# Hybrid decoder block on one core: paired latent tiles, projection norms' roots on GpSimd, and a new load order before the MLP

## The chip, the cores and the metric

One Trainium2 chip, one core of it. The metric is device time in microseconds of one execution; 2975.97 us is the median of 3 runs of the kernel before (2975.77 to 2978.42). Below, TensorE is the matmul engine (PE in the rows, PEld its weight loads), DVE is VectorE, ACT is ScalarE, POOL is GpSimd, and SP issues most loads. DVE and ACT read PSUM, where TensorE writes; GpSimd reads and writes SBUF alone.

## The reference

A transformer block on x of 2048 tokens by 1024, float32, in this order:

- `h = rmsnorm(x, attn_norm_g)`; `proj = h @ w_in`, 2216 columns: the queries, keys and values of 8 Fox heads (3 x 512), 8 forget gates, the query latent c_q (384), the key/value latent c_kv (256), and a rotary key (32).
- Fox: causal attention with a decay bias made from the cumulative sum of `log_sigmoid` of the gates.
- MLA: `c_q` and `c_kv` are normalised (`rmsnorm` over 384 and 256), then multiplied by `w_uq` and `w_ukv`, giving queries, keys and values of 8 heads of 64, and rotary parts of 32; causal attention.
- Both results are normalised and joined; `x = x + mixed @ w_o`.
- `x = x + square(relu(rmsnorm(x) @ w_up)) @ w_down`, 4096 wide, then a final `rmsnorm`.

An rmsnorm needs `1/sqrt(mean(x*x) + eps)` for each token: here "the root".

## The kernel before

**Precision.** Every float32 operand of a matmul is split in a high part and a rest (`split_ps`, `split_w`, `split_to`), and a product is three matmuls (`mm3`, lines 126 to 128): high x high, high x rest, rest x high. Large products are done by seven half-size products of sums instead of eight (names S1 to S4 and T1 to T4 are such sums).

**Slots.** SBUF holds 16 tiles of 8 KB a partition ("big", `s8`) and 21 of 4 KB ("mid", `s4`). Taking a slot takes the one that has been free longest; what writes it first waits for its last reader. PSUM holds four tiles of two banks each (`bank2`).

**Stages.** The projection runs in two rounds of 1024 tokens (p = 0, 1). In each: `prep` normalises an x tile of 128 tokens (squares on ACT, root, scaling on DVE at line 334) and its `turn` transposes it on TensorE (line 339) and splits it. Eight query latents (`latent` with w_cq) and, after the MLA queries, eight key/value latents (with w_ck, 296 columns that include the rotary key and the gates, copied to `krf` at line 389). A latent is 24 matmuls; squares on ACT (385), the root, scaling on DVE out of PSUM (387), and, three `mm3` later, a transpose (394) and a split. Then MLA keys and values (`mla_rows`, `mla_v`), the rotary keys and, in round 1, the gates. Between the latents, `step()` puts halves of the T sums on GpSimd (532, 543). Then `fox`: 21 products, whose last seven (c = 2) in round 0 bring along the eight `prep` of round 1.

After the attention, `fetch` reads a tile of the joined result, and 16 tiles are multiplied by w_o (lines 1087 to 1117; `seq` takes them in pairs from two halves). Each tile ends in a norm, and two of them are turned (`turn`, 1007) and made into the operands of the up products, some kept, some stored in DRAM (`xd`) and loaded again (`x_load`). `x_split` splits such an operand, `up_load` and `up_prep` load and split w_up.

**The root** (`rstd`, 77 to 88): DVE scales and adds eps (79), GpSimd takes the power -1/2 (81), and four DVE instructions (83 to 87) do one Newton step.

**Order.** Each engine runs its own list in order. The lists are made by a planner from a simulated timeline: among instructions that are ready it takes the earliest written. `pin` keeps an instruction behind the one written before it on its engine; the T sums on GpSimd and some splits are pinned. `later(n, f)` runs f after n more `mm3`, and `flush` runs what is due.

Of the kernel before, what the change touches and what calls it, by code (L numbers as in the profile page):

```python
# [18 lines left out]
P = 128  # L19
# [26 lines left out]
def block_kernel(ctx, tc, x, positions, attn_norm_g, w_in, b_forget, q_norm_g, w_uq, kv_norm_g, w_ukv,  # L46
# [30 lines left out]
    def rstd(ssq, n, w=1, tag=""):  # L77
# [9 lines left out]
        nc.vector.tensor_tensor(r, y, t, ALU.mult)  # L87
        return r
# [164 lines left out]
    with ExitStack() as es:  # L253
# [17 lines left out]

        def load_g_att():
            g = s4.get([P, D], F32)
            nc.sync.dma_start(g, attn_norm_g.broadcast_to([P, D]))
            return g
# [52 lines left out]
        def prep(X, t):  # L328
# [5 lines left out]
            nc.vector.scalar_tensor_tensor(xt, xt, rstd(ssq, D, tag="x"), g_att, ALU.mult, ALU.mult)  # L334
# [15 lines left out]
        def load_latent(*cols, early=False):  # L350
# [3 lines left out]
            for half in range(2):  # L354
                hi, lo = s8.get([P, 4, n]), s8.get([P, 4, n])
                parts.append((hi, lo))
                for k in (0, 2):
# [4 lines left out]
                    if early:  # L362
                        nc.scalar.activation(hi[:, k:k + 2], raw, AF.Copy)
                        nc.gpsimd.tensor_tensor(lo[:, k:k + 2], raw, f32v(hi[:, k:k + 2]), ALU.subtract)
                    else:
                        split_w(hi[:, k:k + 2], lo[:, k:k + 2], raw)
# [12 lines left out]
        def latent(X, t, w, n, nn, gain, dst):  # L379
            j, i = t // 4 % 2, t % 4  # L380
            ps = bank2()[:, 0]
            mm3(ps[:, 0:nn], lambda k: [a[:, k % 4, tk(i)] for a in X[f"B{k // 4 + 1}{j + 1}"]],
                lambda k: [a[:, k % 4] for a in w[k // 4]], KD)
            ssq = sml.tile([P, 1], F32, name="ssq")
            nc.scalar.activation(junk_c[:, 0:n], ps[:, 0:n], AF.Square, accum_out=ssq)
            cn = s4.get([P, n], F32)
            nc.vector.scalar_tensor_tensor(cn, ps[:, 0:n], rstd(ssq, n), gain, ALU.mult, ALU.mult)
            if nn > n:
                nc.vector.tensor_copy(krf[:, t], ps[:, n:nn])  # L389

            def turn():
                tp = bank2()[:, 0]
                for k in range(n // P):
                    nc.tensor.transpose(tp[:, tk(k)], cn[:, tk(k)], ident)
                split_ps(dst[0][:, :, tk(i)], dst[1][:, :, tk(i)], tp[:, 0:n].rearrange("p (k s) -> p k s", s=P))
                s4.put(cn)
            later(DEFER_C, turn)
            flush(False)
# [255 lines left out]
        wcq = load_latent((OFF_CQ, RQ), early=True)  # L654
# [3 lines left out]
        def ahead(p, c, i):  # L658

            nonlocal wcq, g_att, first  # L660
            if c < 2:
                return
            if p == 0:
                if i == 0:
                    g_att = load_g_att()
                elif i in (1, 3):
                    prep_operands(Xn, i // 2)
                while turns and i < 6:
                    turns.pop(0)()
                if 1 <= i < 1 + 4:  # L670
                    turns.extend(prep(Xn, 8 + 2 * (i - 1) + n) for n in range(2))
                if i == 5:
# [7 lines left out]
        for p in range(2):  # L680
# [5 lines left out]
            for i in range(8):  # L686
                if p == 0:
# [5 lines left out]
                    if i == 0:  # L693
                        load_constants()
# [3 lines left out]
                latent(X, 8 * p + i, wcq, RQ, RQ, g_q, cq[i // 4])  # L698
# [19 lines left out]
            for i in range(8):  # L718
                latent(X, 8 * p + i, wck, RKV, 296, g_kv, ck[i // 4])
# [14 lines left out]
            mla_rows(g0, ck[0], 2, wk, mk, None)  # L734
            flush()
            for n in range(2):
# [3 lines left out]
            split_operand(X, raws, "T1")  # L740
            mla_rows(g0 + 1, ck[1], 2, wk, mk, None)
            s4.put(*wuk)
            fox_prep(0)
            mla_v(g0, ck[0], wuv)
            s4.put(*ck[0])
# [234 lines left out]
    def fetch(t, first):  # L980
        mt = s4.get([P, KD, P], F32)
        nc.sync.dma_start(mt, mixT.rearrange("(k p) s -> p k s", p=P)[:, :, tk(t)])
        sq = s4.get([P, KD, P], F32)
# [7 lines left out]
        st = [mh, ml]  # L991
# [95 lines left out]
    for n, t in enumerate(seq):  # L1087
        st = cur.pop()
        mh, ml, r2 = st
# [510 lines left out]
```

## Time and profile before

| | |
|---|---|
| median of 3 runs | 2975.97 us |
| the profiled execution | 2976.84 us, its span 2975.0 us |
| TensorE busy | 2825.9 us, 95% of the span |
| DVE, ACT, GpSimd busy | 2276.2, 1399.4, 1350.0 us |
| bytes moved by DMA | 442.96 MB, 149 GB/s |
| granted TensorE clock, mean | 0.979 |

A share of the span is a mean over stages with different limits: in attention and in the MLP TensorE is hardly ever idle, and the idle time lies in the projection, at the start, and around the MLP's first products. The granted clock is given as a share of full speed (2.4 GHz); the lower level is half of it.

### The profile page before, as it was taken

Reading aid. Unit: us, or ns where it says so; the run is one execution under the profiler, and the core shown is the slowest. Engines: PE = TensorE matmul, PEld = TensorE weight load, DVE = VectorE, ACT = ScalarE, POOL = GpSimd, SP = SyncE. Lnnn points to the kernel's source line nnn. Section 1 sums busy time; section 2 is a strip of 40 time slices with the busy share of each in tenths; the row PEclk is TensorE's granted clock in tenths of the full one; section 3 lists DMA queues with packets and bytes.
Section 4 is the critical chain, followed back from the end, with each engine's and each line's share of the span. In section 5 each row is a group of like instructions: output and inputs, shape, how many; then the busy total and the mean of one; then the engine's idle time right before and its main releaser. Section 6 shows DMA issues by size and latency. Waiting matters only on the chain. (4 is left out here: it accounts for less than half of the span.)

```text
span 2975.0 us, 40707 instructions
## 1 busy us (share of the span) xinstructions
PE 2825.9 (95%) x14634; PEld 2375.9 (80%) x14634; DVE 2276.2 (77%) x3317; ACT 1399.4 (47%) x2485; POOL 1350.0 (45%) x896
## 2 busy tenths in 40 slices
PE   7799979999999999999899889999999999999998
PEld 7778968878888888887778778888888788878886
DVE  7867686588888888888757666658666678897998
ACT  4144223477877777787533323223222433344432
POOL 3624252355445545547623235556555433453321
PEclk9999989999999999999999999999999999999999
DMA  5364535834434335331245654455444844465551
GB/s 140 127 217 161 162 108 174 254 90 105 94 89 112 85 91 118 79 90 59 62 146 184 209 197 156 156 211 220 158 152 150 292 153 153 139 219 190 205 191 57
DMA packets 262521, 442.96 MB, mean 149 GB/s; under 512 B 41712, under 2 KB 150384, under 8 KB 255600
## 3 DMA queue, kind: packets, MB, share of 16 engines
q1 hardware_dynamic: 206848, 300.75, 34.3%
q10 hardware_dynamic: 55472, 139.61, 12.4%
q8 instruction: 116, 1.90, 0.3%
q14 instruction: 85, 0.70, 0.1%
HBM read 275.54 MB, written 156.37 MB: 145 GB/s over the span
## 5 line engine op out<-in xcount | busy, mean ns | idle before, releaser
L1257 PE MATMUL mm<-big,mid 128*128 128x512 f32 x2688 | 619.7, 392 | 17.9 <-DVE mid L1038 7.2
L1257 PEld LDWEIGHTS mm<-big,mid 128*128 128x128 f32 x2688 | 505.9, 189 | 130.6 <-ACT big L1332 10.3
L128 PE MATMUL mm<-big,mid 128*128 128x512 f32 x1312 | 513.9, 393 | 7.9 <-DVE mid L237 6.2
L821 PE MATMUL ps_s<-big,big 96*128 96x384 f32 (+11 forms) x1720 | 447.8, 381 | 3.4 <-ACT mid L827 3.4
L127 PE MATMUL mm<-big,big 128*128 128x512 f32 (+2 forms) x1160 | 436.4, 376 | 0.6 <-DVE big L237 0.6
L126 PE MATMUL mm<-big,big 128*128 128x512 f32 (+2 forms) x1072 | 404.4, 377 | 12.3 <-DVE krf L389 9.8
L847 POOL TENSOR_SCALAR mid<-mid,rl,fac 128x768 f32<-128x768 f32 (+4 forms) x256 | 257.8, 1017 | 288.1 <-DVE rl L844 149.5
L826 DVE TENSOR_REDUCE negm<-ps_s 128x1 f32<-128x896 f32 (+7 forms) x384 | 348.3, 908 | 47.7 <-PE ps_s L821 42.9
L243 POOL TENSOR_TENSOR mid<-mid,mid 128x1024 f32<-128x1024 f32 x88 | 237.8, 2702 | 294.6 <-DVE mid L577 94.9
L236 ACT ACTIVATE big<-mid 128x1024 fp32r<-128x1024 f32 x218 | 214.9, 1049 | 319.9 <-PE mm L127 200.5
L827 ACT ACTIVATE mid<-ps_s,negm 128x896 f32<-128x896 f32 (+7 forms) x384 | 332.3, 866 | 50.4 <-DVE negm L826 42.2
L867 PE MATMUL ps_t<-ident,mid 128*128 128x128 f32 x2176 | 341.5, 275 | 4.0 <-POOL mid L847 2.9
L867 PEld LDWEIGHTS ps_t<-ident,mid 128*128 128x128 f32 x2176 | 276.0, 142 | 58.5 <-POOL mid L847 3.1
L821 PEld LDWEIGHTS ps_s<-big,big 96*128 96x128 f32 (+2 forms) x1720 | 291.2, 194 | 20.8 <-ACT mid L827 7.8
L1168 POOL TENSOR_TENSOR mid<-mid,mid 128x1024 f32<-128x1024 f32 x60 | 197.6, 3320 | 230.6 <-DVE big L237 217.2
L128 PEld LDWEIGHTS mm<-big,mid 128*128 128x128 f32 x1312 | 248.1, 189 | 61.2 <-DVE mid L237 7.1
L237 DVE TENSOR_TENSOR mid<-mid,mid 128x1024 fp32r<-128x1024 f32 x112 | 206.1, 1865 | 116.0 <-ACT mid L236 79.7
L94 DVE TENSOR_TENSOR big<-ps_t,big 128x512 fp32r<-128x512 f32 (+3 forms) x427 | 254.4, 602 | 36.6 <-ACT big L93 33.3
L93 ACT ACTIVATE big<-ps_t 128x512 fp32r<-128x512 f32 (+3 forms) x427 | 224.7, 534 | 108.5 <-PE ps_t L867 105.0
L127 PEld LDWEIGHTS mm<-big,big 128*128 128x128 f32 x1160 | 220.9, 190 | 36.5 <-DVE big L237 1.0
L126 PEld LDWEIGHTS mm<-big,big 128*128 128x128 f32 x1072 | 204.1, 190 | 47.0 <-DVE krf L389 10.8
L126 PE MATMUL mm<-big,mid 128*128 128x512 f32 x528 | 210.6, 399 | 7.1 <-ACT mid L988 3.2
(213 smaller groups left out, 5188.3 us busy)
## 6 DMA issues: line engine op xcount, KB each, us to landing
gd<-mid ACTq DMA_DIRECT2D x109, 512.0 KB, 3.0
mid<-gd SPq DMA_DIRECT2D x109, 512.0 KB, 3.6
mid<-in_w_up SPq DMA_DIRECT2D x64, 512.0 KB, 5.3
mid<-in_w_down SPq DMA_DIRECT2D x64, 512.0 KB, 5.1
mid<-in_x SPq DMA_DIRECT2D x32, 512.0 KB, 3.6
xd<-mid ACTq DMA_DIRECT2D x28, 512.0 KB, 3.4
big<-xd SPq DMA_DIRECT2D x14, 1024.0 KB, 8.4
mid<-in_w_in SPq DMA_DIRECT2D x24, 512.0 KB, 4.6
```

The source lines that it names most:

```text
L93: nc.scalar.activation(hi, ps, AF.Copy)
L94: nc.vector.tensor_tensor(lo, ps, f32v(hi), ALU.subtract)
L126: nc.tensor.matmul(ps, lh, rh, start=(k == 0), stop=False)
L127: nc.tensor.matmul(ps, lh, rl, start=False, stop=False)
L128: nc.tensor.matmul(ps, ll, rh, start=False, stop=(k == nk - 1))
L243: (eng or nc.gpsimd).tensor_tensor(t, raws[a], raws[b], op)
L821: nc.tensor.matmul(ps[:, i, 0:wm], l[0:rows, qs], r[0:rows, kb:kb + wm], start=(n == 0), stop=(n == len(ops) - 1))
L826: nc.vector.tensor_reduce(negm[:, j, c:c + 1], src, AX.XY, ALU.max, negate=True)
L827: nc.scalar.activation(prob[:, 0:w].rearrange("p (b w) -> p b w", b=nb), src, AF.Exp, bias=negm[:, j, c:c + 1], accum_out=lsum[:, j, c:c + 1])
L847: nc.gpsimd.tensor_scalar(pr, pr, rl, 1.0 if nch == 1 else fac[:, j, c:c + 1], ALU.mult, ALU.mult)
L867: nc.tensor.transpose(ps[:, j * P:(j + 1) * P], prob[:, kt * P - k0:(kt + 1) * P - k0], ident)
L1257: nc.tensor.matmul(ps[:, m], l[:, k, tk(m)], r[:, :, tk(k)], start=(first and k == n == 0), stop=(k == 3 and n == 2), skip_group_check=True)
```

## The change

- `rstd_pool` does all six instructions of a root on GpSimd. It is used for the x tiles of round 1 (t > 7) and for the latents. The tiles of round 0 and all later norms keep `rstd`.
- `latent` works on pairs: two tiles fill the two halves of one PSUM tile. After the second, ACT copies both halves to an SBUF slot, squares them from there and copies the rotary part to `krf`; one `rstd_pool` of two columns; two scalings on DVE in SBUF; and one `turn` for both, three `mm3` later (eight for the last pair of the key/value latents).
- The first weights are split by ACT and DVE, and after the first two x tiles; before, by ACT and GpSimd, at once.
- The gain and the x tiles of round 1 are loaded in the Fox products c = 1, i = 5 and 6 and then a step ahead of their `prep`.
- `mla_v` of the first half goes ahead of the rotary keys, the gates and `mla_rows` of the second half; the split of T1 and `fox_prep(0)` move with it.
- At w_o, the x tile is loaded in `fetch`, one tile earlier. `up_load(0)` goes from tile 13 to 14; B21's load from tile 11 to the middle of tile 15, when two of the four weight pairs have been given back; the split of T2 from behind the loop to tile 10.

```
+    def rstd_pool(ssq, n, w=1, tag=""):
+        op = nc.gpsimd
+        v, y, t, r = (sml.tile([P, 4], F32, name=f"rp_{c}{tag}")[:, 0:w] for c in "vytr")
+        op.tensor_scalar(v, ssq, 1.0 / n, EPS, ALU.mult, ALU.add)
+        op.tensor_tensor(y, v, mhalf[:, 0:w], ALU.pow)
+        op.tensor_tensor(t, y, y, ALU.mult)
+        op.tensor_tensor(t, t, v, ALU.mult)
+        op.tensor_scalar(t, t, -0.5, 1.5, ALU.mult, ALU.add)
+        op.tensor_tensor(r, y, t, ALU.mult)
+        return r
...
+        def fetch_x(*ts):
+            for t in ts:
+                xts[t] = load_x(t)
...
-            nc.vector.scalar_tensor_tensor(xt, xt, rstd(ssq, D, tag="x"), g_att, ALU.mult, ALU.mult)
+            nc.vector.scalar_tensor_tensor(xt, xt, (rstd_pool if t > 7 else rstd)(ssq, D, tag="x"), g_att, ALU.mult, ALU.mult)
...
-                    if early:
-                        nc.scalar.activation(hi[:, k:k + 2], raw, AF.Copy)
-                        nc.gpsimd.tensor_tensor(lo[:, k:k + 2], raw, f32v(hi[:, k:k + 2]), ALU.subtract)
+                    if splits is None:
+                        split_w(hi[:, k:k + 2], lo[:, k:k + 2], raw)
                     else:
-                        split_w(hi[:, k:k + 2], lo[:, k:k + 2], raw)
+                        splits.append(lambda hi=hi[:, k:k + 2], lo=lo[:, k:k + 2], raw=raw: split_to(hi, lo, raw))
...
+        pair = []
+
+        def latent(X, t, w, n, nn, gain, dst, defer):
             j, i = t // 4 % 2, t % 4
-            ps = bank2()[:, 0]
...
+            a = t % 2
+            if a == 0:
+                pair[:] = [bank2()]
+            ps, = pair
+            mm3(ps[:, a, 0:nn], lambda k: [b[:, k % 4, tk(i)] for b in X[f"B{k // 4 + 1}{j + 1}"]],
+                lambda k: [b[:, k % 4] for b in w[k // 4]], KD)
+            if a == 0:
+                flush(False)
+                return
+            raw = s4.get([P, 2, 512], F32)
+            cn = raw[:, :, 0:n]
+            nc.scalar.activation(raw[:, :, 0:nn], ps[:, :, 0:nn], AF.Copy)
+            ssq = sml.tile([P, 2], F32, name="ssq")
+            for b in range(2):
+                nc.scalar.activation(junk_c[:, 0:n], cn[:, b], AF.Square, accum_out=ssq[:, b:b + 1])
             if nn > n:
-                nc.vector.tensor_copy(krf[:, t], ps[:, n:nn])
+                nc.scalar.activation(krf[:, t - 1:t + 1], raw[:, :, n:nn], AF.Copy)
+            r = rstd_pool(ssq, n, 2)
+            for b in range(2):
+                nc.vector.scalar_tensor_tensor(cn[:, b], cn[:, b], r[:, b:b + 1], gain, ALU.mult, ALU.mult)
...
-            later(DEFER_C, turn)
+            later(defer, turn)
...
+            if p == 0 and c == 1 and i > 4:
+                if i == 5:
+                    g_att = load_g_att()
+                else:
+                    fetch_x(8, 9)
...
+                    if i < 4:
+                        fetch_x(8 + 2 * i, 9 + 2 * i)
...
                     if i == 0:
+                        for f in splits:
+                            f()
                         load_constants()
...
-                latent(X, 8 * p + i, wck, RKV, 296, g_kv, ck[i // 4])
+                latent(X, 8 * p + i, wck, RKV, 296, g_kv, ck[i // 4], DEFER_C if i < 7 else 8)
...
             mla_rows(g0, ck[0], 2, wk, mk, None)
+            split_operand(X, raws, "T1")
+            mla_v(g0, ck[0], wuv)
             flush()
+            s4.put(*ck[0])
             for n in range(2):
                 rotary_keys(g0 + n)
             if p:
                 forget_gates()
-            split_operand(X, raws, "T1")
+            fox_prep(0)
             mla_rows(g0 + 1, ck[1], 2, wk, mk, None)
             s4.put(*wuk)
-            fox_prep(0)
-            mla_v(g0, ck[0], wuv)
-            s4.put(*ck[0])
...
     def fetch(t, first):
+        xt = s4.get([P, D], F32)
+        nc.sync.dma_start(xt, x[tk(t), :])
...
-        xt = s4.get([P, D], F32)
-        nc.sync.dma_start(xt, x[tk(t), :])
+        if n == 14:
+            up_load(0)
...
+            if n == 15:
+                for w in wo[2 * g:2 * g + 2]:
+                    s8.put(*w)
+                if g == 0:
+                    x_load(0, "B21")
...
-        if n == 11:
-            x_load(0, "B21")
-        if n == 13:
-            up_load(0)
+        if n == 10:
+            x_split(0, "T2")
...
-    for w in wo:
-        s8.put(*w)
     up_prep(0, 2)
-    x_split(0, "T2")
```

## Rows read from the trace of the kernel before

**Rows 1.** The page: busy time by engine, one group, one DMA issue (KB, us to landing).
```profile
PE 2825.9 (95%) x14634; PEld 2375.9 (80%) x14634; DVE 2276.2 (77%) x3317; ACT 1399.4 (47%) x2485; POOL 1350.0 (45%) x896
...
L93 ACT ACTIVATE big<-ps_t 128x512 fp32r<-128x512 f32 (+3 forms) x427 | 224.7, 534 | 108.5 <-PE ps_t L867 105.0
...
big<-xd SPq DMA_DIRECT2D x14, 1024.0 KB, 8.4
```

**Rows 2.** Waits of TensorE, whole span: us in total, times, longest.
```profile
PE mm L126 <- DVE krf L389: 24.6, 6, 7.4
PE mm L339 <- DVE mid L334: 17.3, 3, 8.9
...
PE mm L1257 <- DVE mid L1038: 7.2, 1, 7.2
...
PE mm L126 <- ACT mid L93: 6.0, 2, 4.7
...
PE mm L394 <- DVE mid L94: 4.9, 4, 1.5
PE mm L339 <- DVE rs_vx L79: 4.0, 1, 4.0
```

**Rows 3.** Table of stretches: length, busy us by engine, granted clock, DMA share, GB/s.
```profile
85.00:152.00 67.00, 50.88 (x299) 45.29 (x298) 54.66 (x97) 13.29 (x32) 39.34 (x24) 0.87 0.43 141
365.00:446.00 81.00, 59.34 (x320) 51.24 (x320) 67.05 (x129) 20.03 (x43) 42.07 (x25) 0.85 0.38 128
255.00:300.00 45.00, 39.00 (x309) 38.38 (x308) 37.63 (x72) 22.38 (x39) 20.53 (x18) 0.92 0.54 171
```

**Rows 4.** Groups on DVE, 92 to 146 us: busy us, mean ns, idle before.
```profile
L83 DVE TENSOR_TENSOR rs_t<-rs_y 128x1 f32<-128x1 f32 x8 | 15.9, 1982 | 2.8 <-POOL rs_y L81 2.7
...
L387 DVE SCALAR_TENSOR_TENSOR mid<-mm,rs_r,mid 128x256 f32<-128x256 f32 x8 | 3.9, 482 | 0.3
```

**Rows 5.** Groups on GpSimd, whole span.
```profile
L532 POOL TENSOR_TENSOR big<-big,big 128x1024 f32<-128x1024 f32 x16 | 38.1, 2385 | 0.0
...
L81 POOL TENSOR_TENSOR rs_y<-rs_v,mhalf 128x2 f32<-128x2 f32 x16 | 14.3, 891 | 60.8 <-DVE rs_v L79 60.8
...
L847 POOL TENSOR_SCALAR mid<-mid,rl 128x128 f32<-128x128 f32 x16 | 5.9, 370 | 12.9 <-DVE rl L835 12.9
```

**Rows 6.** Timeline of DVE at the start: start us, us, idle before in brackets.
```profile
6.76 0.16 DVE L83 TENSOR_TENSOR rs_tx<-rs_yx 128x1 f32<-128x1 f32 x1 [0.68 <-POOL rs_yx L81]
...
7.54 1.28 DVE L334 SCALAR_TENSOR_TENSOR mid<-mid,rs_rx,mid 128x1024 f32<-128x1024 f32 x1
...
10.25 1.78 DVE L83 TENSOR_TENSOR rs_tx<-rs_yx 128x1 f32<-128x1 f32 x1 [0.67 <-POOL rs_yx L81]
...
15.60 2.79 DVE L334 SCALAR_TENSOR_TENSOR mid<-mid,rs_rx,mid 128x1024 f32<-128x1024 f32 x1
...
29.42 1.02 DVE L104 TENSOR_TENSOR mid<-mid,mid 128x768 fp32r<-128x768 f32 x1
```

**Rows 7.** Timeline of GpSimd at the start.
```profile
10.21 7.10 POOL L364 TENSOR_TENSOR big<-mid,big 128x768 fp32r<-128x768 f32 x4
```

**Rows 8.** Timeline of TensorE: at the start, and after the latents of round 0.
```profile
18.44 1.97 PE L339 MATMUL mm<-ident,mid 128*128 128x128 f32 x8 [7.60 <-DVE mid L334]
...
127.72 0.30 PE L126 MATMUL mm<-big,big 128*128 128x296 f32 x1
...
129.64 0.30 PE L128 MATMUL mm<-big,big 128*128 128x296 f32 x1
...
140.94 0.80 PE L126 MATMUL mm<-mid,mid 128*128 128x512 f32 x1 [7.40 <-DVE krf L389]
...
144.94 0.55 PE L126 MATMUL mm<-mid,mid 128*128 128x512 f32 x1
```

**Rows 9.** Timeline of ACT in the last Fox products of round 0.
```profile
258.21 1.06 ACT L333 ACTIVATE junk<-mid 128x1024 bf16<-128x1024 f32 x1 [2.94 <-DMA mid<-in_x]
```

**Rows 10.** Timeline of DVE on the way into the MLP.
```profile
1688.66 4.48 DVE L237 TENSOR_TENSOR big<-big,big 128x2048 fp32r<-128x2048 f32 x2
```

More of the change, by code (lines that the diff above doesn't have):

```diff
@@ L348, in block_kernel, with load_latent @@
         ukv = w_ukv.rearrange("(k p) (h d) -> p k h d", p=P, d=2 * HD)
-        def load_latent(*cols, early=False):
+        def load_latent(*cols, splits=None):
             n = sum(c[1] for c in cols)
@@ L377, in load_heads @@
             return hi, lo
-        def latent(X, t, w, n, nn, gain, dst):
+        pair = []
+        def latent(X, t, w, n, nn, gain, dst, defer):
             j, i = t // 4 % 2, t % 4
-            ps = bank2()[:, 0]
[L382 to L387, printed above, removed]
+            a = t % 2
[13 more added lines that the diff above has]
+                nc.scalar.activation(junk_c[:, 0:n], cn[:, b], AF.Square, accum_out=ssq[:, b:b + 1])
@@ L388, in latent @@
             if nn > n:
-                nc.vector.tensor_copy(krf[:, t], ps[:, n:nn])
+                nc.scalar.activation(krf[:, t - 1:t + 1], raw[:, :, n:nn], AF.Copy)
+            r = rstd_pool(ssq, n, 2)
+            for b in range(2):
+                nc.vector.scalar_tensor_tensor(cn[:, b], cn[:, b], r[:, b:b + 1], gain, ALU.mult, ALU.mult)
             def turn():
-                tp = bank2()[:, 0]
-                for k in range(n // P):
-                    nc.tensor.transpose(tp[:, tk(k)], cn[:, tk(k)], ident)
@@ L395, in turn @@
-                split_ps(dst[0][:, :, tk(i)], dst[1][:, :, tk(i)], tp[:, 0:n].rearrange("p (k s) -> p k s", s=P))
-                s4.put(cn)
-            later(DEFER_C, turn)
+                tp = bank2()
+                for b in range(2):
+                    for k in range(n // P):
+                        nc.tensor.transpose(tp[:, b, tk(k)], cn[:, b, tk(k)], ident)
+                s2 = slice((i - 1) * P, (i + 1) * P)
+                split_ps(*[d[:, :, s2].rearrange("p k (b s) -> p b k s", b=2) for d in dst],
+                         tp[:, :, 0:n].rearrange("p b (k s) -> p b k s", s=P))
@@ L398, in latent @@
+                s4.put(raw)
+            later(defer, turn)
             flush(False)
@@ L652, in fox @@
             s8.put(uv, gs)
-        wcq = load_latent((OFF_CQ, RQ), early=True)
+        splits = []
+        wcq = load_latent((OFF_CQ, RQ), splits=splits)
         Xn, turns = {}, []
@@ L663, in ahead @@
             if p == 0:
-                if i == 0:
-                    g_att = load_g_att()
-                elif i in (1, 3):
+                if i in (1, 3):
                     prep_operands(Xn, i // 2)
@@ L697, in block_kernel @@
                         turns.pop(0)()
-                latent(X, 8 * p + i, wcq, RQ, RQ, g_q, cq[i // 4])
+                latent(X, 8 * p + i, wcq, RQ, RQ, g_q, cq[i // 4], DEFER_C)
                 if i == 3:
@@ L990, in fetch @@
         s4.put(mt)
-        st = [mh, ml]
+        st = [mh, ml, xt]
         def stats():
@@ L1088, in block_kernel @@
         st = cur.pop()
-        mh, ml, r2 = st
+        mh, ml, xt, r2 = st
         if n + 1 < NT:
             cur.append(fetch(seq[n + 1], False))
-        xt = s4.get([P, D], F32)
-        nc.sync.dma_start(xt, x[tk(t), :])
+        if n == 14:
+            up_load(0)
         for g in range(2):
```

## The prediction, made before the changed kernel was run

> **What bounds the kernel now.** I read the page first, then the waits of TensorE, then a table by stage, then the engines' timelines around the longest waits. On the page TensorE is busy for 2825.9 us of 2975.0, DVE for 77% [rows 1]; the reader is to see that at most 149 us of idle TensorE can be won, and that no matmul is taken out here. The view of waits says where the idle time lies [rows 2]. Its first line, 24.6 us in six waits, is a projection matmul that waits for the DVE copy into krf: the last reader of the PSUM tile that the matmul is to write. The next, 17.3 us in three, is the transpose of a normalised x tile that waits for DVE, nearly all of it at the start of the kernel. Both stand in stretches that the change rewrites. The table by stage [rows 3] shows it from the other side: in the two stretches around the key/value latents (85 to 152 us and 365 to 446 us) TensorE is busy for 50.88 of 67 and 59.34 of 81 us, at granted clocks of 0.87 and 0.85, while DVE is busy for 54.66 and 67.05. DVE is late there, though not with its own work: in the first round, the first product of the reciprocal root (128x1) takes 1982 ns on average [rows 4], nearly as long as the GpSimd add of 2385 ns [rows 5] that runs beside it, where the same form takes 0.16 us at 6.76 us, with GpSimd idle [rows 6].
>
> The profiled execution took 2976.84 us, 1.84 us around its span; the median of the runs shown is 0.87 us lower. The sum is made against the execution and moved by 0.87 at the end.
>
> **Part 1, the start.** Before, GpSimd subtracts the four low parts of the first weights in one block of 7.10 us [rows 7]. The second x tile goes from L83 to the end of L334 from 10.25 to 18.39, 8.14 us; the first, beside an idle GpSimd, from 6.76 to 8.82, 2.06 us [rows 6]. The change puts the four subtractions on DVE, behind the two tiles. The block goes and with it 6.1 us of delay. In its place DVE has four subtractions at 1.02 us (the 128x768 form at 29.42 [rows 6]), 4.1 us, half of which I let TensorE's first tile hide, since it takes the weights part by part. Late next is DVE with these low parts. Between 0 (all on the path, and the splits of x behind them) and 7.6 (the wait itself [rows 8]) I take 4.5.
>
> **Part 2, the query latents.** Per tile DVE loses five small instructions, and TensorE hardly waits there. Between -2 and +2: 1.
>
> **Part 3, the key/value latents, two rounds.** Removed: the waits 24.6 (krf), 4.9 (transposes for DVE) and 6.0 (rows for ACT), 35.5 us in all [rows 2]. ACT now copies both halves of a paired PSUM tile at once, and a 512-wide read of PSUM takes it 534 ns [rows 1]; so the tile no longer waits for the norm. With the waits goes slow clock: after the wait that ends at 140.94, nine matmuls take 4.00 us [rows 8] where the later spacing of 0.24 us would take 2.1 (512 columns, from the 296-column spacing below); 1.9 us each for some three such waits in the two rounds, 6 us (bounds 3.8 and 9.5, two and five waits).
>
> Added: a chain that is longer for a pair. ACT copies and squares, three instructions at up to 0.53, about 1.7 us. GpSimd then does six small instructions: the power at 891 ns [rows 5], and five for which the nearest row is the 128x128 scaling, 370 ns, so 2.7 us (at 0.1 us each it would be 1.4). GpSimd also has two pinned adds per pair, 4.8 us, each placed behind the roots in front of it. A pair costs it 7.5 us, and TensorE 48 matmuls at 0.137 us (fifteen from 127.72 to 129.64 [rows 8]), 6.6 us, plus four transposes. They are about even, so a root can find an add in front of it. Then come two scalings on DVE. Before, one took 482 ns [rows 4] whatever GpSimd did; its tile came from PSUM. Now both inputs lie in SBUF, as with the product that takes 1982 ns. The transposes are due three groups of 24 matmuls later, 9.9 us; the last pair has eight groups of six 512-column matmuls, 48 x 0.237 = 11.4 us. Without any add in the way the chain is 1.7 + 2.7 + 1.0 = 5.4 us and hidden; with one add, and both scalings held for 2, it is 1.7 + 2.4 + 2.7 + 5 = 11.8, late by 1.9 for three pairs and 0.4 for the last, 6 us a round. I take 12 for both rounds (bounds 0 and 31, worked out with the first rival). Part 3 gives 35.5 + 6 - 12 = 29.5 (bounds 8.3 and 45).
>
> The value projection goes ahead of the second half of the keys as cover for the last pair. The key rotation, the forget gates and the first split of Fox weights move with it and issue the same instructions and stores; I set them at nothing, hidden by the 24 matmuls of the moved value projection. If that cover is gone, they cost some of the 6.0 that is counted above.
>
> Here the Trainium skill speaks against the change. "SBUF — State Buffer", section "Who interferes with whom": a DVE instruction with two SBUF inputs and a GpSimd instruction that reads SBUF exclude one another for the whole instruction, and one with at most one SBUF input doesn't contend. The trace agrees (1982 against 482 ns). By that rule moving the scaled tile from PSUM to SBUF gives back part of what the product's move wins; the first rival below is what it would cost.
>
> **Part 4, the x tiles of the second half.** TensorE is idle for 6.0 us between 255 and 300 [rows 3], 4.0 of them for the first root [rows 2]. That root is late because ACT waited 2.94 us for an x tile [rows 9]. The tiles and the gain are now asked for up to three products ahead, on the same SP queue, past nothing but the next latents' weights, if their tiles are free by then; the roots leave DVE. GpSimd is busy 20.53 of 45 us [rows 3] and gets at most 8 x 2.7 = 21.6 more: nearly full, but not over. Late next: DVE with the splits. I take 6, clock included (bounds -3 and 9).
>
> **Part 5, the way into the MLP.** The longest wait there is 7.2 us, for DVE's L1038 [rows 2], and right in front of that group DVE does two splits of 128x2048 in 4.48 us [rows 10]. One of them (T2) moves four tiles up, into a loop in which TensorE had no long wait. That takes 2.2 us from the wait. The x loads one tile earlier hide nothing that showed; w_up's first four loads, asked for one tile (11.4 us of TensorE) later, keep the last two tiles as cover. B21's two loads are put back behind the first release of output weights: 8.4 us each to landing [rows 1], against 24 matmuls of the last tile and 24 of the first product, 48 x 0.237 = 11.4 us. They just fit. I take 2.5 (bounds -6 and 7).
>
> **Sum.** 4.5 + 1 + 29.5 + 6 + 2.5 = 43.5; 2976.84 - 43.5 - 0.87 = 2932.5 us. All bounds at their worst together lose 2.7 (2978.7), all at their best win 70.6 (2905.4).
>
> **The rivals.**
> First, the shared port and the full GpSimd: each root waits for two adds, 4.8, and both scalings for one more each: 1.7 + 4.8 + 2.7 + 5 = 14.2, late by 4.3 for three pairs and 2.8 for the last, 15.7 a round, 31 for two. Part 3 gives 10.5, the sum 24.5: 2951.5 us. For it: the product's 1982 ns is already nearly a whole add. Against it: a late TensorE lets GpSimd run empty. Chance 0.22.
>
> Second, the MLP's loads: if B21's two transfers run one after the other, 16.8 us, TensorE waits 5.4 us and the 2.5 are lost: 2932.5 + 8 = 2940. For it: w_up's first loads stand in front of them in the same queue. Against: 8.4 us is the median of fourteen such issues, most of them in pairs. Chance 0.11.
>
> Third, slower: GpSimd's small instructions cost 0.9 us each, as the 128x2 power does, not 0.37. A root chain is 5.4 us, a pair 10.2 against TensorE's 7.2: 3 us more for eight pairs, 24, on top of the first rival's 31; part 3 gives -13.5. In part 4 a product brings two chains and a subtraction, 13.2 us, against some 7.5 of TensorE: 23 us over four products, part 4 gives -17. Sum 4.5 + 1 - 13.5 - 17 + 2.5 = -22.5: 2998 us. It decides from about 0.6 us an instruction. Against it: 370 ns for 64 times as many columns. Chance 0.07.
>
> Fourth, it doesn't do what it says: the engines' orders are made anew from estimated times, and TensorE waits elsewhere for as long: 2970 to 2982. Against it: the waits of part 3 have one cause, and that cause is gone. Chance 0.08.
>
> **How the numbers follow.** The forecast has 0.52, with its own range 2918 to 2947. The range of 2910 to 2962 leaves out the third and fourth rivals and a little beyond the first. Within 0.2%, about what a measurement of this kernel can tell from no change, is +-6 us. Faster: 0.52 + 0.22 + 0.11 = 0.85; same: the fourth, 0.08; slower: the third, 0.07.
>
> **What would show it.** Right: no wait for krf or for a reader of the latents' PSUM tile; granted clock in both key/value stretches above 0.93; L83 gone from them; the second x tile's transposes near 12 us; GpSimd's root chain near 2.7 us for two columns. Wrong in part 3: transposes of the latents that wait for the scaling, 3 us or more each. Wrong in part 5: a matmul of the first MLP products waiting for xd. The prediction falls if the key/value stretches shorten by less than 10 us together, or if a GpSimd root instruction takes over 0.6 us.

## The result: 2932.9 us, by other terms than predicted

The changed kernel takes 2932.9 us (median of four runs, 2932.1 to 2933.6), the kernel before 2977.2 us beside it (2975.8 to 2981.5): a ratio of 0.9849, 95% interval 0.9832 to 0.9866, or 44.3 us. Forecast were 2932.5. The total is right, and its parts are not: the key/value latents gave some 11 us where 29.5 were forecast, and the way into the MLP some 21 us where 2.5 were.

The lead of the changed kernel's TensorE over that of before, at the same point of the work, shows it (from the two profiled executions, us):

| point | before | after | lead |
|---|---|---|---|
| first query latent | 20.06 | 16.85 | 3.2 |
| last query latent of round 0 | 64.66 | 59.99 | 4.7 |
| first key/value latent of round 0 | 93.03 | 89.44 | 3.6 |
| first Fox product of round 0 | 166.97 | 156.09 | 10.9 |
| end of the second Fox stage of round 0 | 247.50 | 232.42 | 15.1 |
| first query latent of round 1 | 303.59 | 284.90 | 18.7 |
| first key/value latent of round 1 | 366.84 | 349.07 | 17.8 |
| first Fox product of round 1 | 447.35 | 425.79 | 21.6 |
| first score of the attention | 558.49 | 539.42 | 19.1 |
| last score | 1453.76 | 1428.38 | 25.4 |
| first MLP product | 1695.91 | 1653.70 | 42.2 |
| end of the up products | 2339.59 | 2293.48 | 46.1 |

Some steps of the lead are in no term of the forecast: 4.2 us in the first two Fox stages of round 0 (10.9 to 15.1; TensorE's waits of 2.1 us for the splits of Fox weights are gone there), 6.3 us in the attention, and 2.0 and 2.5 us lost on the ways to the key/value latents and behind the first Fox product of round 1.

Below, a key/value stretch is the time from the first latent of 296 columns to the first Fox product. Before, the two took 73.9 and 80.5 us; after, 66.7 and 76.7.

First the page of the changed kernel, and below it the waits of TensorE over the whole span (us in total, times, longest), to hold against [rows 1] and [rows 2].

```profile
PE 2808.3 (96%) x14634; PEld 2365.1 (81%) x14634; DVE 2220.2 (76%) x3089; ACT 1413.7 (48%) x2493; POOL 1371.5 (47%) x996
...
L105 ACT ACTIVATE big<-ps_t 128x512 fp32r<-128x512 f32 (+3 forms) x427 | 225.0, 534 | 108.4 <-PE ps_t L907 101.0
...
big<-xd SPq DMA_DIRECT2D x14, 1024.0 KB, 8.8
```

```profile
PE mm L355 <- DVE mid L350: 13.9, 3, 9.4
...
PE mm L424 <- DVE mid L418: 10.2, 6, 2.0
PE mm L138 <- DVE big L106: 9.1, 2, 6.9
PE mm L138 <- DVE mid L106: 7.6, 4, 2.5
PE mm L1054 <- DVE mid L1153: 7.2, 4, 2.8
```

The two waits that the change was to remove, for krf (24.6) and for L1038 (7.2), are gone. In their place stand three that were absent or small before: transposes of the latents that wait for their scaling (L418), matmuls that wait for the evictions of rows and values (L106, DVE's part of taking a product out of PSUM), and the turn transposes of the output projection, which wait for DVE's L1153. The page shows TensorE busy for 17.6 us less, though the matmuls are the same 14634; with it the mean granted clock rose from 0.979 to 0.986.

Now the key/value stretches, in the table of stretches: length, busy us by engine, granted clock, DMA share, GB/s. The kernel before from its own first latent to its first Fox product (rounds 0 and 1):

```profile
93.00:167.00 74.00, 58.19 (x315) 50.65 (x314) 59.18 (x97) 19.63 (x42) 42.39 (x25) 0.88 0.42 146
366.80:447.40 80.60, 59.25 (x315) 51.09 (x314) 66.65 (x122) 21.43 (x44) 43.30 (x25) 0.85 0.37 129
```

The same two of the changed kernel:

```profile
89.40:156.10 66.70, 54.91 (x315) 48.08 (x314) 46.45 (x46) 22.51 (x46) 47.14 (x40) 0.95 0.48 164
349.10:425.80 76.70, 58.39 (x315) 49.45 (x313) 59.26 (x72) 26.13 (x51) 46.72 (x41) 0.90 0.42 144
```

DVE has 12.7 and 7.4 us less to do, GpSimd 4.8 and 3.4 more. TensorE still stands idle for 11.8 and 18.3 us, where it was 15.8 and 21.4.

What holds it is seen on DVE in round 0: groups (busy us, mean ns, idle before) from 85 to 152 us, to hold against [rows 4], and then its timeline (start, us, idle before in brackets).

```profile
L418 DVE SCALAR_TENSOR_TENSOR mid<-mid,rp_r,mid 128x256 f32<-128x256 f32 x8 | 13.6, 1744 | 2.4 <-POOL rp_r L99 2.4
...
L496 DVE TENSOR_TENSOR big<-krf,mid 128x128 f32<-128x128 f32 x2 | 2.7, 1334 | 0.2 <-PE mm L139 0.2
```

```profile
101.02 1.23 DVE L116 TENSOR_TENSOR mid<-mid,mid 128x1024 fp32r<-128x1024 f32 x1 [1.54 <-POOL mid L113]
104.14 3.42 DVE L116 TENSOR_TENSOR mid<-mid,mid 128x1024 fp32r<-128x1024 f32 x1 [1.89 <-POOL mid L113]
109.30 2.94 DVE L418 SCALAR_TENSOR_TENSOR mid<-mid,rp_r,mid 128x256 f32<-128x256 f32 x2 [1.74 <-POOL rp_r L99]
112.89 5.10 DVE L418 SCALAR_TENSOR_TENSOR mid<-mid,rp_r,mid 128x256 f32<-128x256 f32 x2 [0.64 <-POOL rp_r L99]
...
125.13 0.87 DVE L418 SCALAR_TENSOR_TENSOR mid<-mid,rp_r,mid 128x256 f32<-128x256 f32 x2
```

The reader is to see one instruction, the scaling of 128x256, at three prices. The fourth line holds two of them in 5.10 us, the last line two in 0.87 (the pair after it, at 129.75, takes 4.72 again). The timeline of GpSimd in the same stretch says why:

```profile
101.07 1.23 POOL L94 TENSOR_SCALAR rp_v<-ssq 128x2 f32<-128x2 f32 x1
102.38 0.70 POOL L95 TENSOR_TENSOR rp_y<-rp_v,mhalf 128x2 f32<-128x2 f32 x1
103.06 1.05 POOL L113 TENSOR_SCALAR mid<-mid 128x1024 fp32r<-128x1024 f32 x1
104.07 2.41 POOL L575 TENSOR_TENSOR big<-big,big 128x1024 f32<-128x1024 f32 x1
106.44 1.17 POOL L96 TENSOR_TENSOR rp_t<-rp_y 128x2 f32<-128x2 f32 x1
...
109.06 0.20 POOL L99 TENSOR_TENSOR rp_r<-rp_y,rp_t 128x2 f32<-128x2 f32 x1
...
112.80 2.41 POOL L575 TENSOR_TENSOR big<-big,big 128x1024 f32<-128x1024 f32 x1
115.16 2.55 POOL L564 TENSOR_TENSOR big<-big,big 128x1024 f32<-128x1024 f32 x1
```

The two scalings of 5.10 us stand beside two adds, 112.80 to 117.71; those of 0.87 beside none. The first pair's root chain, 2.1 us when nothing is between, takes 8.2 (101.07 to 109.26): a weight copy (L113) and an add (L575) stand between its second and third instruction. It also goes the other way: GpSimd's L94 and L96, 0.19 and 0.21 us in the round's last chain, take 1.23 and 1.17 while DVE's subtraction of two SBUF inputs (L116, 128x1024) runs.

At the end of the second stretch another wait has come, 6.88 us. In one fence each: TensorE at the first Fox product, DVE and GpSimd in front of it (DVE's first line is an earlier subtraction with no GpSimd instruction beside it).

```profile
425.79 0.79 PE L138 MATMUL mm<-big,mid 128*128 128x512 f32 x1 [6.88 <-DVE big L106]
```

```profile
401.91 1.22 DVE L589 TENSOR_TENSOR big<-big,big 128x1024 fp32r<-128x1024 f32 x1
...
417.34 4.52 DVE L589 TENSOR_TENSOR big<-big,big 128x1024 fp32r<-128x1024 f32 x2 [1.55 <-ACT big L588]
421.78 3.35 DVE L609 TENSOR_TENSOR mid<-mid,mid 128x1024 fp32r<-128x1024 f32 x1
425.06 2.47 DVE L106 TENSOR_TENSOR big<-mm,big 128x512 fp32r<-128x512 f32 x4
```

```profile
414.92 9.13 POOL L255 TENSOR_TENSOR mid<-mid,mid 128x1024 f32<-128x1024 f32 x3 [16.73 <-DMA krd<-big]
```

The four evictions of the values (L106, one SBUF input, 0.62 us each) stand in DVE's order behind the split of T2 and of a Fox weight, and these stand beside three Fox combines on GpSimd (sums of Fox weights, L255): 4.52 us for two and 3.35 for one, where one of this form takes 1.22 alone.

The way into the MLP, DVE first: before, T2 and another operand of 128x2048 stood in front of the last evictions of the output projection [rows 10]. After, one is left there:

```profile
1655.11 3.46 DVE L249 TENSOR_TENSOR big<-big,big 128x2048 fp32r<-128x2048 f32 x1
...
1664.22 3.47 DVE L1153 SCALAR_TENSOR_TENSOR mid<-mid,rs_r,g_m 128x1024 f32<-128x1024 f32 x1
```

The second line is the scaling for which the turn transposes now wait. It has two inputs in SBUF and takes 3.47 us beside weight sums on GpSimd (L255, 1654.01 to 1666.60); the median of its sixteen is 1.28.

### The profile page after: what moved, and what is told of

It is laid out like the page before. It is cut to its first block, busy times and chain, and to the rows that moved or that the text cites. A ratio compares the mean times of both kernels' runs of the same rounds, so it can differ in the third digit from the quotient of the medians.

```text
span 2930.3 us, 40573 instructions
## 1 busy us (share of the span) xinstructions
PE 2808.3 (96%) x14634; PEld 2365.1 (81%) x14634; DVE 2220.2 (76%) x3089; ACT 1413.7 (48%) x2493; POOL 1371.5 (47%) x996
## 5 line engine op out<-in xcount | busy, mean ns | idle before, releaser
L248 ACT ACTIVATE big<-mid 128x1024 fp32r<-128x1024 f32 (+1 forms) x222 | 218.3, 1046 | 322.4 <-PE mm L139 193.7
L255 POOL TENSOR_TENSOR mid<-mid,mid 128x1024 f32<-128x1024 f32 x88 | 241.2, 2741 | 262.2 <-DVE mid L249 112.6
L140 PEld LDWEIGHTS mm<-big,mid 128*128 128x128 f32 x1312 | 248.1, 189 | 62.1 <-DVE mid L249 7.5
L249 DVE TENSOR_TENSOR mid<-mid,mid 128x1024 fp32r<-128x1024 f32 x112 | 193.3, 1754 | 117.4 <-ACT mid L248 83.4
L106 DVE TENSOR_TENSOR big<-ps_t,big 128x512 fp32r<-128x512 f32 (+3 forms) x427 | 254.2, 602 | 28.6 <-ACT big L105 25.0
```

Of the source, the lines that this page charges most:

```text
L106: nc.vector.tensor_tensor(lo, ps, f32v(hi), ALU.subtract)
L140: nc.tensor.matmul(ps, ll, rh, start=False, stop=(k == nk - 1))
L255: (eng or nc.gpsimd).tensor_tensor(t, raws[a], raws[b], op)
```

## Experiments

Two questions. Why did part 3 give a third of its term, and where did part 5's 20 us come from? Theory P says that the scaling is held by the adds, since it now has two inputs in SBUF; theory G that GpSimd is full and the roots come late; theory D that DVE's own order at the end of a stretch is at fault. For part 5, theory A has the gain in its own edits, theory B in the projections' new timing.

The table has all kernels: median us, ratio to the kernel before on the same chip with its interval, and of the profiled execution four times in us: the two key/value stretches (KV0, KV1), the handover to the output projection (W, from the last score to its 145th matmul, the end of three tiles), and from its last tile's first matmul to the 193rd MLP matmul (M).

| kernel | median | ratio (95%) | KV0 | KV1 | W | M |
|---|---|---|---|---|---|---|
| before | 2977.2 | 1 | 73.9 | 80.5 | 76.8 | 77.7 |
| after | 2932.9 | 0.9849 (0.9832 to 0.9866) | 66.7 | 76.7 | 69.8 | 63.8 |
| e1 projections only | 2962.0 | 0.9949 (0.9936 to 0.9961) | 66.2 | 77.9 | 76.6 | 84.6 |
| e2 MLP way only | 2959.0 | 0.9934 (0.9920 to 0.9948) | 74.0 | 79.5 | 71.2 | 64.2 |
| e3 x tile early | 2964.6 | 0.9953 (0.9939 to 0.9966) | 74.1 | 81.2 | 70.2 | 72.9 |
| e4 order and split | 2969.3 | 0.9969 (0.9957 to 0.9980) | 74.5 | 80.9 | 76.5 | 62.2 |
| e5 scaling from PSUM | 2922.9 | 0.9811 (0.9796 to 0.9827) | 59.0 | 65.9 | 71.2 | 62.2 |
| e6 roots on DVE | 2939.7 | 0.9868 (0.9852 to 0.9885) | 71.2 | 69.9 | 76.3 | 62.3 |
| e7 T2 after values | 2929.6 | 0.9830 (0.9815 to 0.9844) | 66.7 | 70.5 | 70.6 | 62.4 |
| e8 no sums | 2911.7 | 0.9765 (0.9741 to 0.9789) | 54.7 | 56.1 | 72.8 | 64.4 |
| e9 e5 and e7 | 2920.9 | 0.9801 (0.9781 to 0.9821) | 59.4 | 66.4 | 71.4 | 62.2 |
| e10 e9, copies on ACT | 2917.3 | 0.9792 (0.9770 to 0.9814) | 59.0 | 63.3 | 70.1 | 62.1 |
| e11 MLP's T2 late | 2945.5 | 0.9891 (0.9870 to 0.9913) | 64.9 | 77.4 | 69.6 | 69.8 |
| e12 part 4 undone | 2935.0 | 0.9852 (0.9832 to 0.9873) | 66.7 | 71.4 | 73.2 | 62.8 |

One caution for all of them: the attention, which no edit touches, takes 889.0 to 896.3 us from first to last score over these kernels, 889.0 in the changed kernel and 895.3 in the one before. I can't put that down to an edit, so differences of a few us between single executions are read from the stretches and not from the end.

### Which half of the change

e1 is the kernel before with parts 1 to 4, e2 with part 5 alone; both are hunks of the diff and nothing else.

> Parts 1 to 4 of the change alone; the output projection and the way into the MLP stay as before. Theory A (the gain is local: about 19 us by the start of the attention, 4 to 5 more inside the attention, 22 on the way into the MLP): the attention starts near 539 us as in the changed kernel, the first MLP product keeps its wait of 7 us, and the time is 2953 us (2950 to 2957). Theory B (the shorter way into the MLP comes with the projections, because the engines meet the handover in another order): 2933 to 2940 us. The prediction's own terms (41 us of the 43.5 in parts 1 to 4): 2935 us.

> Part 5 of the change alone: x tile asked for with the mixed tile, first w_up loads one tile later, result weights freed in halves, B21 loaded behind the first half, T2 split after tile 10. Theory A: the attention starts where it started before (558 us), TensorE gains 22 us between the last score matmul and the first MLP product, and the time is 2953 us (2950 to 2957). Theory B: at most 5 us gained, 2971 us or above. The prediction's own term: 2.5 us, 2973.5 us.

Measured: 16.8 us by parts 1 to 4, 19.9 by part 5. Theory B falls, and so do the prediction's own terms (41 and 2.5). Theory A is right in kind, and too simple: it expected 2953 us of each, the halves make 36.7 us and the whole 44.3. The last column shows where most of the other 7.6 are: with part 5 undone, parts 1 to 4 take 6.9 us longer into the MLP than before (84.6 against 77.7), and part 5 takes that away too (63.8).

### Which edit on the way into the MLP

e3 is the kernel before with the x tile loaded in `fetch`, beside the mixed tile:

```
         mt = s4.get([P, KD, P], F32)
         nc.sync.dma_start(mt, mixT.rearrange("(k p) s -> p k s", p=P)[:, :, tk(t)])
+        xt = s4.get([P, D], F32)
+        nc.sync.dma_start(xt, x[tk(t), :])
...
-        xt = s4.get([P, D], F32)
-        nc.sync.dma_start(xt, x[tk(t), :])
```

e4 is the kernel before with the rest of part 5: w_up's first loads at tile 14, the output weights freed in halves, B21's loads behind the first half, T2 split after tile 10.

> The kernel before with one edit of part 5: the x tile is asked for together with the mixed tile, one tile earlier. If the gain at the handover (first ten tiles of the output projection, 10 us) comes from this load, 10 us faster, 2966 us, with the wait of 7 us at the first MLP product still there. If the x tile was hidden anyway, as the prediction held: 2976 us, within 3.

> The kernel before with the rest of part 5: w_up's first loads at tile 14, halves of the output weights freed one by one, B21's loads behind the first half, T2 split after tile 10; the x tile is asked for as before. If the last two tiles and the first MLP products are where the gain is: 12 us faster, 2964 us, and no wait of 7 us at the first product. If the two loads of B21 come too late (second rival), a matmul of the second product waits 5 us and the time is 2973 to 2978 us.

Measured: 14.2 us and 9.5 us. The columns part them. W falls by 6.6 us with the x tile (76.8 to 70.2) and not without it (76.5), M by 15.5 us with order and split (62.2) and by 4.8 with the x tile. W is 76.5 to 76.8 in the three kernels with the late load and 69.6 to 73.2 in those with the early one, but for e6 (76.3), where the reason is open. So "the x loads one tile earlier hide nothing that showed" was wrong. They showed in a view that I had not read, the waits of SP's queue, here of the kernel before from 1450 to 1535 us (L1093 is the x tile's load, L989 the subtraction that frees a mixed tile, L984 its square):

```profile
SPq L1093 <- DVE mid L989: 12.6, 2, 7.3
...
SPq L1093 <- DMA mid<-mixT: 7.8, 2, 4.4
...
SPq L1093 <- ACT mid L984: 1.2, 1, 1.2
```

All three write or read the next mixed tile: the x tile took the place in SBUF that this one gives up, so its load waited until it had landed and been split. That is 21.6 us in five waits in front of three loads, in a queue in which the next loads stand behind. Taken one tile earlier the x tile gets another place; after, no load of one (L1024) waits for a mixed tile, though they still wait 13.4 us for a store and a norm's scaling of other tiles (from 1415 to 1500 us). TensorE's own waits in the first three tiles fall by little, from 10.9 to 8.0 us in the two kernels; the rest of W's 7.0 us goes with the clock, 0.94 granted over W before and 0.98 after.

e3 falls short of e4 in M: waits of the MLP products remain in it, 4.3, 2.9, 1.1, 0.5 and 0.2 us, while e4 has none of them. The 7-us wait is in neither: in e3 it went though its T2 is late, which e3's expectation had excluded.

e11 is the changed kernel with T2 split where it was:

```
-        if n == 10:
-            x_split(0, "T2")
...
     up_prep(0, 2)
+    x_split(0, "T2")
     up_prep(0, 3)
```

> The changed kernel, but the T2 operand of the MLP is split behind the last tile of the output projection, as before the change; load order, halves of the weights and the early x tile stay. If the early split is what shortens the way into the MLP: the wait of 7 us for the pair's evictions is back, with slow clock behind it, and the time is 2943 us (2940 to 2947). If the load order alone does it: 2933, within 3.

Measured: 2945.5, 12.6 us slower than the changed kernel; the intervals don't meet (0.9870 to 0.9913 against 0.9832 to 0.9866). The early split is needed; the expected time was met (2940 to 2947), but the loss has not the expected form. TensorE waits for other evictions, from 1600 to 1760 us:

```profile
PE mm L1298 <- ACT big L1373: 4.8, 1, 4.8
PE mm L1298 <- ACT mid L248: 1.8, 1, 1.8
```

M is 6.0 us longer; the profiled execution was this kernel's shortest (2939.3), the other four 2944.7 to 2951.2, and what makes them longer no trace shows. If the gains add up, which nothing here tests, 4.8 of the 13.9 us of M come with the x tile (e3) and 6.0 with T2's early split; the load order and the freed halves, which would share the remaining 3, I did not try apart.

### What holds part 3

e5 is the changed kernel with one operand moved:

```
-  nc.vector.scalar_tensor_tensor(cn[:, b], cn[:, b], r[:, b:b + 1], gain, ALU.mult, ALU.mult)
+  nc.vector.scalar_tensor_tensor(cn[:, b], ps[:, b, 0:n], r[:, b:b + 1], gain, ALU.mult, ALU.mult)
```

> The changed kernel, but the two scalings of a pair read the latents from the PSUM tile instead of the copy in SBUF. Theory P (the missing gain of part 3 is the scaling that is held while GpSimd adds): the key/value scalings fall from 1.5 to 1.7 us on average to 0.5, the transposes' waits for them (5.2 and 5.0 us in the two key/value stretches of the changed kernel) fall to about 1, and the time is 2924 us (2920 to 2929). Theory G (GpSimd is full, the roots are late): the scalings are short but start as late, and the time stays at 2933, within 3. A rival on the other side: the PSUM tile is held until the norm is done, and the wait for its last reader, 24.6 us in the kernel before, comes back in part: 2938 us or above.

Measured: 2922.9. Its DVE group and its two stretches:

```profile
L418 DVE SCALAR_TENSOR_TENSOR mid<-mm,rp_r,mid 128x256 f32<-128x256 f32 x8 | 3.5, 479 | 6.3 <-POOL rp_r L99 6.3
```

```profile
91.00:150.00 59.00, 54.35 (x315) 48.43 (x313) 34.46 (x43) 22.38 (x46) 45.93 (x40) 0.94 0.54 183
346.60:412.40 65.80, 56.53 (x314) 49.27 (x313) 44.98 (x70) 24.23 (x49) 40.30 (x39) 0.90 0.50 169
```

1744 ns became 479, no transpose waits for a scaling any more, and the stretches lose 7.7 and 10.8 us. Against the kernel before they are 15.0 and 14.6 us shorter, 29.6 together. That part 3 was to give 29.5 is chance: without held scalings its own sum would be 41.5, and 12.2 us of waits for evictions (L106) remain, which are in no term. By the time it is 10 us and not 18.5. Most of the difference lies in front of the key/value stretches: from the first query latent to the first key/value latent e5 takes 1.8 and 2.6 us longer than the changed kernel. The three kernels that scale from PSUM (e5, e9, e10) have the longest such ways of all fourteen, 74.0 to 75.1 and 65.3 to 66.9 us against 71.2 to 73.6 and 63.2 to 64.3. In e5 the transposes of the MLA queries wait 6.3 us for DVE's L476, where it was 3.5; whether the held PSUM tile is behind it is not shown. At the first score the lead over the changed kernel is 14.4 us, and the 4.4 that are lost behind it are less than the scatter named above. Theory P stands. No wait for the reader of the held PSUM tile shows.

e6 puts `rstd` back for the pairs (`r = rstd(ssq, n, 2)`).

> The changed kernel, but the latents' reciprocal roots are the mixed chain again, power on GpSimd and the rest on DVE, for a pair at a time. Theory P: the products of two SBUF inputs on DVE wait for the adds, 2 us each in four pairs of two rounds, some 10 us lost, 2943 us. Theory G: GpSimd gains 1.4 us a pair and the time falls to 2928 us. If where the roots run doesn't matter: 2933, within 3.

Measured: 2939.7. Its groups on DVE in round 0 (87.8 to 159 us):

```profile
L83 DVE TENSOR_TENSOR rs_t<-rs_y 128x2 f32<-128x2 f32 x4 | 9.4, 2346 | 1.6 <-POOL rs_y L81 1.6
L84 DVE TENSOR_TENSOR rs_t<-rs_t,rs_v 128x2 f32<-128x2 f32 x4 | 7.9, 1970 | 0.1
...
L85 DVE TENSOR_SCALAR rs_t<-rs_t 128x2 f32<-128x2 f32 x4 | 5.0, 1245 | 0.1
L418 DVE SCALAR_TENSOR_TENSOR mid<-mid,rs_r,mid 128x256 f32<-128x256 f32 x8 | 4.6, 612 | 0.1
```

The adds hold whichever of the chain's instructions comes first: the roots now wait (2346 ns for two columns), the scaling hardly. KV0 grows by 4.5 us, as P says. KV1 shrinks by 6.8, because the collision at its end doesn't happen, and W, which the edit doesn't touch, is 6.4 us longer. The two stretches together are 2.3 us shorter, where P expected 10 lost, and the intervals of the two kernels overlap (from 0.9852 here, to 0.9866 there): the time is near P's 2943, but the rows show P in KV0 alone.

e7 moves one line, `split_operand(X, raws, "T2")`, behind `mla_v(g0 + 1, ck[1], wuv)` and the two `put`s that follow it.

> The changed kernel, but T2 is split behind the second value projection instead of in front of it. Theory D (the longest wait left in the second key/value stretch, 6.9 us for the evictions of the values, is DVE's T2 split, 4.5 us, and the Fox split, 3.4 us, held by four GpSimd combines): that wait falls below 3 us and the time to 2928 us (2926 to 2931). Rival: T2 then comes too late for the fourth Fox product, which waits for as long: 2933 us or above.

Measured: 2929.6, 3.3 us below the changed kernel, with intervals that overlap. KV1 falls from 76.7 to 70.5, and the wait in front of the first Fox product from 6.88 to 0.32 us. Theory D holds for that place. No Fox product waits for T2. The same collision is absent in e12 (KV1 71.4), which differs only far ahead of it: so it seems to depend on where GpSimd's combines happen to fall.

e8 leaves the sums of the x operands out on GpSimd (sixteen a round, not the twelve of the expectation; the operands T are then not the reference's, and a load stands in the place of eight of them):

```
-  pin(nc.gpsimd.tensor_tensor(raws[old][:, ks], raws[a][:, ks], raws[b][:, ks], op))
...
-  pin(nc.gpsimd.tensor_tensor(raws[q][:, ks], f32v(X[q][0][:, ks]), f32v(X[q][1][:, ks]), ALU.add))
+  nc.sync.dma_start(raws[q][:, ks], win[:, ks, 0:512])
```

> The changed kernel without the sums of the x operands on GpSimd (B and T, twelve a round are left out; loads of as many bytes of the projection weights stand in their place, so the operands T are not those of the reference). Theories P and G together: the key/value stretches (66.7 and 76.7 us in the changed kernel) lose 15 to 18 us in sum, as much as part 3 fell short, and the time is 2916 us. Theory D alone: the first stretch loses 3 us, the second keeps its waits for evictions, and the time is 2928 us or above.

Measured: 2911.7, 21.2 us below the changed kernel.

```profile
90.00:144.70 54.70, 52.33 (x315) 46.81 (x314) 26.85 (x44) 21.71 (x45) 17.38 (x29) 1.00 0.72 246
337.60:393.60 56.00, 53.24 (x314) 47.66 (x313) 32.26 (x69) 23.91 (x48) 12.21 (x28) 0.97 0.71 244
```

The stretches fall by 32.6 us, twice what P and G together had foreseen. The sums so cost the changed kernel 32.6 us of its two stretches, though no matmul there waits for GpSimd directly. 18.5 of it is the scaling (e5). The other 14 I did not take apart; beside an add stand also the late roots, the splits of weights and the rotation (L496, 1334 ns in the changed kernel, 288 here).

### A version that beats both, and part 4

e9 has e5 and e7 together. e10 adds the first rounding of two weights on ACT (`load_heads` hands the name on to `split_w`):

```
-  wuk = load_heads(2, ukv, 0, HD, 0, H)
-  wuv = load_heads(2, ukv, HD, 2 * HD, 0, H)
+  wuk = load_heads(2, ukv, 0, HD, 0, H, "act")
+  wuv = load_heads(2, ukv, HD, 2 * HD, 0, H, "act")
```

> The changed kernel with both edits that won: the scaling reads the PSUM tile, and T2 is split behind the second value projection. If the two costs are separate (port in the first three quarters of a key/value stretch, T2's split at the end of the second): 10 + 3 us below the changed kernel, 2920 us (2916 to 2923), the stretches 59 and 60 us. If they are one and the same lateness of DVE: no better than the scaling alone, 2923 to 2926 us.

> The kernel of both edits, and the first rounding of the key and value up-projection weights (two copies of 128x1024 a round, 1.05 us each, which stand between the first pair's root instructions on GpSimd) goes to ACT. If the first pair's root chain, 8.1 us in the changed kernel against 2.1 for the last, is what remains of the first key/value stretch: 2 us a round, 2916 us. If ACT then waits for these weights with the pair's PSUM copies behind it: 2923 us or above.

Measured: 2920.9 and 2917.3. Both beat the changed kernel, whose interval they don't touch; among e5, e9 and e10 the intervals overlap. In e9, KV1 is 66.4, no shorter than e5's 65.9: once the scaling is off the shared port, the collision that e7 removes is no longer late, so the two costs were one lateness there. e10's KV1 is 3.1 us shorter than e9's, its KV0 0.4.

e12 undoes part 4: `rstd` for all x tiles, the loads and the gain where they were.

> The changed kernel without part 4: the x tiles and the gain of the second half are loaded where they were, and their roots are the mixed chain on DVE and GpSimd. By the prediction's term 6 us slower, 2939 us. By the traces, in which the two kernels differ by 3.6 us between the end of the second Fox stage and the second query latents: 2937 us. If both hide behind the Fox products anyway: 2933, within 3.

Measured: 2935.0, no difference that the intervals could show. The stage itself is 4.1 us longer (56.6 against 52.5 us from the end of the second Fox stage to the second query latents), and the wait of 4.3 us for rs_vx is back; KV1 then gives 5.3 back.

## Why the prediction was right in the sum and wrong in its parts

**Parts 1 and 2** were 5.5 us; the lead at the end of the first query latents is 4.7. The mechanism is as described, with one detail off. The second tile's transposes start at 15.23 and not near 12, since two of DVE's four splits and an eviction stand between the second root's instructions, and a third split in front of the scaling, and not behind both tiles. This is DVE and TensorE there:

```profile
10.37 0.96 DVE L249 TENSOR_TENSOR big<-mid,big 128x768 fp32r<-128x768 f32 x1
...
11.43 0.96 DVE L249 TENSOR_TENSOR big<-mid,big 128x768 fp32r<-128x768 f32 x1
...
12.36 0.68 DVE L106 TENSOR_TENSOR big<-mm,big 128x512 fp32r<-128x512 f32 x1
12.96 0.15 DVE L87 TENSOR_TENSOR rs_rx<-rs_yx,rs_tx 128x1 f32<-128x1 f32 x1
13.03 0.95 DVE L249 TENSOR_TENSOR big<-mid,big 128x768 fp32r<-128x768 f32 x1
13.90 1.28 DVE L350 SCALAR_TENSOR_TENSOR mid<-mid,rs_rx,mid 128x1024 f32<-128x1024 f32 x1
```

```profile
15.23 1.97 PE L355 MATMUL mm<-ident,mid 128*128 128x128 f32 x8 [3.87 <-DVE mid L350]
```

**Part 3** is the step that failed: 29.5 forecast, 11.1 measured, and the first rival's 10.5 was close. What was removed went: no wait for krf, L83 gone from the stretches. What failed is the term "12 for both rounds", which took one add in the way of a root and 2 us for each scaling. The runs put 18.5 us on the scalings alone. For the wait of the transposes, which is all that the term counted, 12 was not far off (10.2 us measured); left out were the evictions of rows and values that DVE reached late, 16.7 us (12.2 of them are left in e5, with the scalings free). The clock stayed low with it, at 0.95 and 0.90 where more than 0.93 was called for in both. The stretches are 11.1 us shorter together, just above the 10 at which the prediction was to fall. No transpose waited 3 us, so my own sign for "wrong in part 3" did not fire: there are six waits of at most 2.0 us for a scaling, and six for the evictions. The loss of a held engine shows here in many waits, most of them small.

The Trainium skill, "SBUF — State Buffer", section "Who interferes with whom", was drawn on for this, and priced as the minor case. The trace bears its rule out (1744 ns with both inputs in SBUF, 479 with one in PSUM, 482 without adds). My restatement left out its exception: in a two-port mode a copy or a tensor_scalar with a single SBUF input contends as well. The changed kernel may have such a case on DVE in round 1, two tensor_scalar instructions of one input and one shape, the first beside an add, the second not; in which mode they ran no trace shows:

```profile
388.97 2.27 DVE L529 TENSOR_SCALAR mid<-mid 128x128 f32<-128x128 f32 x1
...
401.76 0.23 DVE L527 TENSOR_SCALAR mid<-mid 128x128 f32<-128x128 f32 x1
```

"I set them at nothing" for the moved key rotation, forget gates and first Fox split was wrong for round 1 by up to 6 us: with them goes the place at which T2's split meets the combines (e7). This was only tried by moving T2, not by undoing the move. On the other side stand the 4.2 us won in the Fox stages of round 0, and which edit won them was not tried.

**Part 4** was 6 us; the stage gave 3.6. Undoing it costs 2 us, less than the intervals can tell from nothing. The wait for the first root (rs_vx, 4.0 us) went as described; in its place TensorE waits 3.2 us for an addition on DVE (L666), which the sum did not have and which is not there in e12.

**Part 5** is the other step that failed, 2.5 forecast. Alone it is 19.9 us, with the other parts some 27. Two sentences of it did: the x tile "hides nothing that showed" (6.6 us of W and 4.8 of M by e3), and T2's split was priced at its own 2.2 us, when it also ends a row of waits and the lower clock behind them (6.0 us of M by e11, granted 0.91 over M there and 0.97 in the changed kernel; the time is 12.6 longer, and where the rest goes is not shown). The second rival did not occur: B21's loads made no MLP product wait.

**The rivals.** The first has the right number for part 3 and not for the total; its transposes, late by 2.8 to 4.3 us each, did not occur (2.0 at most), so its number is in part chance too. The third fell: for two columns GpSimd's power takes 0.70 us and the other five 0.19 to 0.22 (medians), 2.1 a chain that nothing interrupts. By the letter the last sign, a root instruction of over 0.6 us, was met all the same, by the power and by others that took up to 1.2 us beside DVE; it can't have been meant for the power, which the sum had at 0.89. The total came out because one term was 18 too large and another some 18 too small; that is luck, and the range of 2910 to 2962 was wide enough for either alone.

## What to carry to other kernels

Where two engines hold each other up, as DVE and GpSimd do here, look at which operands a moved instruction reads, and not only at its length: one operand left in PSUM was worth 18 us of two stretches here, and some 10 of the time. A load can start only when its place in SBUF is free, so the queue's own waits have to be read before a load is called hidden (here 21.6 us of them). A stage with short waits and a lower clock holds more than its longest wait.

## What was not expected of the hardware

GpSimd is held as well as DVE: two of its instructions of 128x2 took 1.17 and 1.23 us beside a DVE subtraction of two SBUF inputs, 0.19 to 0.22 in the median. And the sums on an engine that is busy for 47% of the span, and for which no matmul of the two stretches waits directly, cost 32.6 us there (e8), by holding DVE and by the late roots together.
